# Last quarter of the residual and last head's queries computed by features; arriving tiles in buffers of their own

## The chip, the core and the metric

The kernel runs on one core of one Trainium2 chip. The metric is the device time of one execution in microseconds; the runs given are the median of three, with the lowest and highest. All inputs and outputs are float32.

## What is computed

One encoder block over 256 rows of 2048 features, with a second input of 256 memory rows. Cut to its core:

```python
h = rms_norm(x, norm_g[0])
q, k, v, g, lr, u_f, u_h, u_s = jnp.split(h @ w_in, split_at, axis=-1)
mix = concat([gla(...), rms_norm(fnet(u_f)), rms_norm(hyena(u_h)), rms_norm(shortconv(u_s))])
x = x + mix @ w_out                                                     # 2048 -> 2048
x = x + cross_attention(rms_norm(x, norm_g[1]), mem_n, w_xq, w_xkv, w_xo)
x = x + swiglu(rms_norm(x, norm_g[2]), w_gate_up, w_down)               # 2048 -> 2 x 5632 -> 2048
return rms_norm(x, final_norm_g)

def cross_attention(h, mem_n, w_q, w_kv, w_o):                          # 4 heads of 512
    q = h @ w_q;  k, v = split(mem_n @ w_kv)
    p = softmax(q k^T * 512 ** -0.5);  return (p v) @ w_o
```

## The kernel before

**Three matmuls for one product.** Every float32 operand is split in a high part (a copy to the type fp32r, by ScalarE) and a low part (the difference, by VectorE). A product is high x high + high x low + low x high. A weight block is 128 x 128; weights come in slabs of 16 blocks (1 MB) by one SyncE queue, in the order in which they are used, and are split half a slab (8 blocks) at a time: `Stream._half`, L104 on ScalarE and L105 on VectorE. A half is cast up to two or three halves ahead of its use; the buffers are three (four while `st.extra` is open). Activations lie as 128 features x 256 rows, high part and low part beside each other in one tile of 512 columns: `act[0..23]` and, for a while, others.

**By rows, by features.** A gemm has two forms. By rows (`gemm_rows`, `part_rows`, L347 to L349): the activation is the stationary operand, four weight blocks side by side are the moving one, and the result in PSUM is 128 rows x 512 output features, for each half of the 256 rows. For a group of four blocks that is six matmuls of 512 columns. By features (`gemm`, `mm`, L298 and L299): the weight block is stationary, the activation moves (high and low in one matmul of 512 columns, then the low weights with the high activation, 256 columns), and the result is 128 output features x 256 rows, in two halves which `merge` adds: a copy by ScalarE and an add by VectorE. For four blocks that is eight matmuls, of 3072 columns in all like the six.

**Turning.** A result by rows has its features along the free axis, and the next gemm wants them on partitions. So it is turned: VectorE transposes 32 x 32 blocks (`store_turned`, L382), GpSimd's queue stores the tile to DRAM (L384), and later loads it with the blocks put in their places (`load_turned`, L389). This is done for the residual after `w_out` and after `w_xo` (`features1`, `features2`), for the queries (`queries`), the keys and the MLP's hidden activations. The weights' rows are permuted on the host to fit (`turned`).

**Background work.** While the gemms are written out, small pieces of other work are put between the matmuls by `Background`: each is a generator that yields the time, in microseconds of matmul time counted by the program, after which it may go on. `arrive(src, c, put, ok)` is the piece of this change: it takes four temporaries of 128 x 256, issues the four loads of quarter c, yields 9.0, waits for `ok`, and then splits the four tiles (`put`). Each engine runs its own instructions in order, so a split that is queued too early stands at the head of its engine's queue until its tile has landed, and whatever comes behind it, weight splits too, stands with it. GpSimd's queue too is in order: a load waits there for its stores to land, and what is behind waits as well. The temporaries are a pool of 11 (`tmp`).

**The stages around the change**, in the order in which they run:

- `out_proj`: `w_out` by rows in quarters of 512 features, the first two together, then the third, then the fourth. After each, `add_rows` adds the result into the residual `res[c]` (rows x 512 features), turns and stores it, and squares it on ScalarE for the row norm (`sq`). The slots of `act[16:24]` hold the mixers' output until `w_out` ends, and take the third and fourth quarter of the next input `h2` then.
- `attention`: `w_xq` by rows, one head of 512 queries at a time; each is stored, loaded and split into `q` tiles (eight buffers). Keys and values come from DRAM as `mr` tiles (`load_kv`), and are split into `kt`, `vh`, `vl`. `head` does scores (L776, L777), softmax, and probabilities by values (L803, L804). The first `w_xq` gemm runs over k in parts, 0 to 7, 8 to 11 and 12 to 15, each part behind the arrival of its slots. `row_norm(0)` sums `sq` for the scale.
- `w_xo` by rows, again two quarters together, then one, then one; the third input `h3` arrives as `h2` did.
- `gate_up` and `down`: the MLP, by rows. The first gate_up gemm takes k 0 to 11, then 12 to 15. The final norm needs the residual at the end; its fourth quarter is put into two PSUM banks early (L872: the residual split in two, times the identity `identr`, held through gate_up), and `w_down`'s last quarter is added onto it there.

The lists `late` and `self.late` hold the arrivals; `drain` writes out what is left of one.

Of the kernel before, what the change touches and what calls it, by code (L numbers as in the profile page):

```python
# [22 lines left out]
P = 128  # L23
# [15 lines left out]
ROWS = ((0, 512), (704, 768), (880, 944), (1152, NBLK))  # L39
# [3 lines left out]
LAG, OWED, SOON = 1.3, 0.9, 0.01  # L43
# [19 lines left out]
class Stream:  # L63
# [13 lines left out]
    def _half(self):  # L77
# [24 lines left out]
        edges = [0, 256, 512, 1024] if n == 0 else [0, 512, 1024] if n == 8 else [0, 1024]  # L102
# [69 lines left out]
class Block:  # L172
# [219 lines left out]
    def run(self):  # L392
# [9 lines left out]
        self.identr = cp.tile([P, P], F32R, name="identr")  # L402
# [28 lines left out]
        nc.gpsimd.tensor_copy(self.identr, self.ident)  # L431
        with self.tc.tile_pool(name="wx", bufs=1) as st.extra:
            self.mixers()
            self.attention()
# [6 lines left out]
    def mixers(self):  # L441
# [79 lines left out]
        with tc.tile_pool(name="mid", bufs=1) as mid:  # L521
# [37 lines left out]
            with tc.tile_pool(name="glp", bufs=1) as glp:  # L559
# [13 lines left out]
                self.out_proj(lambda n: self.bg.drain((g_gla, g_sc, g_fn)[n]))  # L573
# [63 lines left out]

    def row_norm(self, n, box):

        self.bg.dve(8)  # L640
        c = self.rp.tile([P, 8], F32, name="sm", tag="sm")[:, 0:2]
        self.nc.vector.tensor_reduce(out=c, in_=self.sq[n].rearrange("p (r k) -> p r k", k=4), axis=AX.X, op=ALU.add)
        box["col"] = self.rstd_cols(c, D)

    def out_proj(self, before):
        nc, act = self.nc, self.act

        def ready(n):

            if n:  # L650
                before(n - 1)
                for c in ((2, 3), (1,), (0,))[n - 1]:
                    for r in range(2):
# [3 lines left out]
        slots = act[4:8] + act[0:4] + act[16:24]  # L657
        h2 = self.h2 = act[8:24]
        put = lambda k, t: self.split_scaled(h2[k], t, self.gvec(V_NG + 16, k))
        free = self.st.n + 192 + 32  # L660
        self.late = []

        def done(c, ps):
            self.add_rows(0, c, ps)
            self.late.append(self.bg.add(self.arrive(self.xf[0], c, put, c > 1 and (lambda: self.st.n >= free)), go=True))

        for c, ps in enumerate(self.gemm_rows("w_out", [0, 512], slots, parts=[range(k, k + 4) for k in (8, 0, 12, 4)], before=ready)):
            done(c, ps)
# [3 lines left out]
    def attention(self):  # L672
        tc, nc, act, st = self.tc, self.nc, self.act, self.st
        with tc.tile_pool(name="atp", bufs=1) as atp, tc.tile_pool(name="kp", bufs=1) as kp, \
# [4 lines left out]
            self.gap(vp, 128)  # L679
            oex = [atp.tile([P, 512], F32R, name=f"oex{i}") for i in range(4)]  # L680
# [13 lines left out]
            heads = []  # L694
# [37 lines left out]
            def scores(hd):  # L732
                q = []

                def put(k, t):
                    q.append(slot("q", 8))
                    self.split(q[-1], t)

                yield from self.arrive(self.qf, hd, put, lambda: len(heads) > hd - 2)
                while len(kv[hd][2]) < 2:  # L740
                    yield
                yield
                yield from self.head(q, *kv[hd], pt, o[4 * hd:4 * hd + 4], qs)
# [4 lines left out]
            late = self.late  # L748
            for hd in range(4):
                first = dict(parts=[range(8), range(8, 12), range(12, 16)],  # L750
                             before=lambda n: [self.bg.drain(g) for g in late[:n + 2]]) if hd == 0 else {}
                for r, p in enumerate(self.gemm_rows("w_xq", [hd * 512], self.h2, **first)[0]):
# [3 lines left out]
            self.late = []  # L756
            put = lambda k, t: self.split_scaled(h3[k], t, self.gvec(V_NG + 32, k))

            def done(c, ps):
                self.add_rows(1, c, ps)  # L760
                self.late.append(self.bg.add(self.arrive(self.xf[1], c, put), go=True))

# [771 lines left out]
```

## Time and profile before

| | |
|---|---|
| runs | 1490.69, 1495.62, 1498.5 us; median 1495.62 us |
| profiled execution | 1493.05 us, its span 1491.2 us |
| mean granted TensorE clock | 0.996 |
| instructions in the span | 18456 |
| DMA | 315.46 MB, mean 212 GB/s |
| GpSimd's queue: stores of residual / loads of residual | 32 / 32, 128 KB each |
| GpSimd's queue: stores of queries / loads of queries | 16 / 16, 128 KB each |

The span runs from the first to the last instruction; the time is a little longer. Times below are microseconds from the span's start. A row of the timeline gives start, duration, engine, line, operation, and in brackets the engine's idle time before it with what ended it. PE is TensorE's matmuls, PEld its weight loads, which overlap them, ACT ScalarE, DVE VectorE, POOL GpSimd and SP SyncE. The stages: `w_out` runs from about 457 to 551, the queries and heads from there, `w_xo` from about 662 to 764 (its first part with the last heads between), `gate_up` behind it to about 1243, and `down` to the end.

### The profile page before, as it was taken

To read this page: it belongs to the slowest core of one execution; us is meant where nothing else is said; L and a number is where in the kernel's file an instruction comes from. 1 tells how busy PE (TensorE), PEld (TensorE's weight loads), DVE (VectorE), ACT (ScalarE), POOL (GpSimd) and SP (SyncE) were. 2 spreads that over 40 slices of the span, in tenths; PEclk is the share of its full clock that TensorE was granted. 3 is DMA by queue.
4 is the path that set the end of the run, shared out by engine and by line. 5 is a ranking of instruction groups with operands and counts; after the bars stand their busy time and mean duration, and the time that the engine had idled before them with its cause. 6 is when DMAs were issued, how large, how long until landed. Compare 5 with 4: busy or idle time off the path is not lost.

```text
span 1491.2 us, 18456 instructions
## 1 busy us (share of the span) xinstructions
PE 1468.3 (98%) x6960; PEld 1223.7 (82%) x6960; DVE 926.5 (62%) x1324; ACT 752.1 (50%) x1092; POOL 172.3 (12%) x229
## 2 busy tenths in 40 slices
PE   9999999999999999999999999999999999999997
PEld 7887888898898877788878888888888888888886
DVE  6668768779767565776664545555554556444444
ACT  6557655467555454665554444444444445444344
POOL 0000000000001324340331001111100111000000
PEclk9999999999999999999999999999999999999999
DMA  9776654454536767774676667666666666555554
GB/s 357 279 273 244 212 203 156 165 185 155 194 141 219 241 210 244 219 218 149 223 244 207 212 212 225 219 216 219 219 214 213 225 214 220 191 194 197 197 195 144
DMA packets 58441, 315.46 MB, mean 212 GB/s; under 512 B 8781, under 2 KB 10478, under 8 KB 26736
## 3 DMA queue, kind: packets, MB, share of 16 engines
q1 hardware_dynamic: 46496, 281.11, 54.9%
q0 software_dynamic: 11424, 32.52, 8.3%
q8 instruction: 54, 0.88, 0.3%
q10 hardware_dynamic: 432, 0.66, 0.1%
q14 instruction: 35, 0.29, 0.1%
HBM read 295.90 MB, written 18.35 MB: 211 GB/s over the span
## 4 chain that ended last, share of the span: by engine, by line
PE 84%; DMA 6%; issue 5%; DVE 2%; POOL 2%; ACT 1%; SPq 0%; POOLq 0%; DVEq 0%; ACTq 0%
PE pg L348 21%; PE pg L347 21%; PE pg L349 21%; PE pg L298 6%; PE pg L299 4%; DMA tmp<-features 2%; DMA features<-tmp 2%; PE pm L349 1%; PE pm L347 1%; PE pm L348 1%; DVE wl L105 1%; PE pg L295 1%; PE pg L296 1%; PE pm L1028 1%; POOL tmp L389 1%
## 5 line engine op out<-in xcount | busy, mean ns | idle before, releaser
L105 DVE TENSOR_TENSOR wl<-raw,wh 128x1024 fp32r<-128x1024 f32 (+1 forms) x503 | 610.2, 1216 | 449.4 <-ACT wh L104 448.2
L104 ACT CAST wh<-raw 128x1024 fp32r<-128x1024 f32 (+1 forms) x503 | 522.8, 1042 | 546.0 <-PE pg L349 456.3
L347 PE MATMUL pg<-wh,act 128*128 128x512 f32 (+1 forms) x1522 | 594.5, 391 | 6.6 <-ACT wh L104 4.0
L348 PE MATMUL pg<-wl,act 128*128 128x512 f32 (+1 forms) x1522 | 593.6, 390 | 3.0 <-DVE wl L105 3.0
L349 PE MATMUL pg<-wh,act 128*128 128x512 f32 (+1 forms) x1522 | 592.9, 390 | 0.4 <-DVE act L204 0.4
L347 PEld LDWEIGHTS pg<-wh,act 128*128 128x128 f32 x1522 | 286.0, 188 | 69.8 <-ACT wh L104 5.2
L348 PEld LDWEIGHTS pg<-wl,act 128*128 128x128 f32 x1522 | 286.0, 188 | 64.8 <-DVE wl L105 6.4
L349 PEld LDWEIGHTS pg<-wh,act 128*128 128x128 f32 x1522 | 286.0, 188 | 61.0 <-DVE act L204 1.5
L299 PE MATMUL pg<-act,wl 128*128 128x256 f32 x512 | 143.5, 280 | 0.0
L298 PE MATMUL pg<-act,wh 128*128 128x512 f32 x400 | 141.2, 395 | 0.0
L299 PEld LDWEIGHTS pg<-act,wl 128*128 128x128 f32 x512 | 96.3, 188 | 0.3
L298 PEld LDWEIGHTS pg<-act,wh 128*128 128x128 f32 x400 | 75.2, 188 | 16.2
L384 POOL DMA_DIRECT2D hidden<-u x22 | 16.7, 762 | 387.1 <-DVE u L382 387.1
L347 PE MATMUL pg<-wh,f 128*128 128x512 f32 x120 | 46.7, 389 | 0.0
L348 PE MATMUL pg<-wl,f 128*128 128x512 f32 x120 | 46.7, 389 | 0.0
L349 PE MATMUL pg<-wh,f 128*128 128x512 f32 x120 | 46.7, 389 | 0.0
L389 POOL DMA_DIRECT2D tmp<-hidden x44 | 38.8, 888 | 39.5 <-ACT wh L104 17.1
L384 POOL DMA_DIRECT2D features<-tmp x32 | 22.7, 715 | 113.0 <-DVE tmp L382 112.5
L204 DVE SCALAR_TENSOR_TENSOR act<-tmp,vec,act 128x256 fp32r<-128x256 f32 x32 | 14.7, 481 | 33.7 <-ACT act L212 33.7
L212 ACT ACTIVATE act<-tmp,vec 128x256 fp32r<-128x256 f32 x32 | 15.4, 504 | 37.2 <-DMA tmp<-features 37.1
L389 POOL DMA_DIRECT2D mr<-keys x16 | 14.2, 890 | 154.1 <-DVE act L200 148.1
L389 POOL DMA_DIRECT2D tmp<-features x32 | 28.1, 885 | 31.2 <-DMA features<-tmp 19.9
(295 smaller groups left out, 1239.2 us busy)
## 6 DMA issues: line engine op xcount, KB each, us to landing
raw<-in_W SPq DMA_DIRECT2D x246, 1024.0 KB, 5.1
raw<-in_W SPq DMA_DIRECT2D x11, 512.0 KB, 7.4
hidden<-u POOLq DMA_DIRECT2D x22, 256.0 KB, 3.6
tmp<-hidden POOLq DMA_DIRECT2D x44, 128.0 KB, 4.9
features<-tmp POOLq DMA_DIRECT2D x32, 128.0 KB, 3.6
tmp<-features POOLq DMA_DIRECT2D x32, 128.0 KB, 5.2
k<-in_mem SPq DMA_DIRECT2D x8, 256.0 KB, 9.0
keys<-k POOLq DMA_DIRECT2D x8, 256.0 KB, 7.2
```

What stands on the lines that cost most here:

```text
L104: nc.scalar.copy(wh[:, a:b], r[:, a:b])
L105: nc.vector.tensor_tensor(out=wl[:, a:b], in0=r[:, a:b], in1=wh[:, a:b].bitcast(F32), op=ALU.subtract)
L212: self.nc.scalar.activation(slot[:, 0:R], src, AF.Copy, scale=g)
L295: self.nc.tensor.matmul(p[:, 0:R], wh, slot[:, 0:R], start=start, stop=False)
L296: self.nc.tensor.matmul(p[:, 0:R], wh, slot[:, R:512], start=False, stop=False)
L298: self.nc.tensor.matmul(p[:, :], wh, slot[:, :], start=start, stop=False)
L299: self.nc.tensor.matmul(p[:, 0:R], wl, slot[:, 0:R], start=False, stop=stop)
L347: self.nc.tensor.matmul(p, hi, wh, start=start, stop=False)
L348: self.nc.tensor.matmul(p, hi, wl, start=False, stop=False)
L349: self.nc.tensor.matmul(p, lo, wh, start=False, stop=stop)
L384: self.nc.gpsimd.dma_start(to[r], u.rearrange("p (k c) -> p k c", c=P))
L389: self.nc.gpsimd.dma_start(t.rearrange("p (g t) -> p g t", t=32), src)
```

## The change

1. The fourth quarter of `w_out` and of `w_xo` is computed by features (`add_features`, L298 and L299): four columns of 16 blocks, each merged and added onto `resk(12 + i)`, which now holds that quarter of the residual as 128 features x 256 rows, loaded from `xT` at the start. No turn, store or load. Squares are summed over the four tiles, and `row_norm` sums them over the partitions with two matmuls by a column of ones. Their splits read the sum in place.
2. The fourth head's queries are computed by features too; the merged tiles are split into `act[12:16]` at its turn. The `q` buffers are four instead of eight, and a head's queries may be split as soon as the head before has been scored.
3. `arrive` takes its tiles from buffers of their own (eight `ar` tiles in `attention`, four in `gate_up`; the third quarter after `w_out` uses `tmp` still), and yields 18.0 (`FAR`) instead of 9.0 between loads and splits. The third quarter after `w_out` is split only when all of `w_out` has been issued.
4. The third quarter after `w_xo` is loaded from the start of `gate_up`, with 11.0 before its splits; the first gate_up gemm runs over k in the parts 0 to 7, 8 to 11 and 12 to 15.
5. The fourth quarter is put into the two PSUM banks only before `down`, by eight transposes; `identr` goes.
6. The third and fourth half slab of the kernel are split in two pieces each (`n < 32`), as the first two were.
7. The weights' permutations and the placement of weight tiles (`ROWS`) follow.

```diff
-ROWS = ((0, 512), (704, 768), (880, 944), (1152, NBLK))
+ROWS = ((0, 512), (704, 768), (880, 944), (1152, 1344), (1408, 1600), (1664, 1856), (1920, NBLK))
-LAG, OWED, SOON = 1.3, 0.9, 0.01
+LAG, OWED, SOON, FAR = 1.3, 0.9, 0.01, 18.0
...
-        edges = [0, 256, 512, 1024] if n == 0 else [0, 512, 1024] if n == 8 else [0, 1024]
+        edges = [0, 256, 512, 1024] if n == 0 else [0, 512, 1024] if n < 32 else [0, 1024]
...
-    def arrive(self, src, c, put, ok=None):
+    def arrive(self, src, c, tile_, put, wait, ok=None):
         m = []
         for k in range(4 * c, 4 * c + 4):
-            m.append(self.tmp())
+            m.append(tile_())
             self.load_turned(m[-1], src, k)
-        yield 9.0
+        yield wait
...
+    def add_features(self, w, slots, h, g):
+        nc = self.nc
+        def add(i, p):
+            x = self.resk(12 + i)
+            self.tt(x, x, self.merge(p), ALU.add)
+            s = self.tmp()
+            nc.scalar.activation(s, x, AF.Square)
+            if i:
+                self.tt(s, self.sqf, s, ALU.add)
+            self.sqf = s
+        def rest():
+            for k in range(12, 16):
+                self.split_scaled(h[k], self.resk(k), self.gvec(g, k))
+                yield SOON
+        self.gemm(w, [1536 + i * P for i in range(4)], slots, add)
+        return self.bg.add(rest())
+
     def row_norm(self, n, box):
-        self.bg.dve(8)
+        nc = self.nc
+        p = self.bank()
+        for r in range(2):
+            nc.tensor.matmul(p[:, r:r + 1], self.sqf[:, r * P:(r + 1) * P], self.ones[:, 0:1], start=True, stop=True)
+        self.bg.dve(8, 2)
...
+        nc.vector.tensor_reduce(out=c, in_=self.sq[n].rearrange("p (r k) -> p r k", k=4)[:, :, 0:3], axis=AX.X, op=ALU.add)
+        self.tt(c, c, p[:, 0:2], ALU.add)
...
+                    if c == 3:
+                        self.load_x(12, 4)
+                        continue
...
-        for c, ks in ((2, [range(16)]), (3, [range(8, 16), range(8)])):
-            done(c, self.gemm_rows("w_out", [c * 512], slots, parts=ks)[0])
...
+            arrival = lambda: mp.tile([P, R], F32, name="ar", tag="ar", bufs=8)
+            free = self.st.n + 128
...
+                late.append(self.bg.add(self.arrive(self.xf[0], c, self.tmp if c > 1 else arrival, put, FAR, c > 1 and (lambda: self.st.n >= free)), go=True))
+            done(0, ps[0])
+            done(1, ps[1])
+            done(2, self.gemm_rows("w_out", [1024], self.mix)[0])
+            late.append(self.add_features("w_out", self.mix, h2, V_NG + 16))
...
-                    q.append(slot("q", 8))
+                    q.append(act[k] if hd == 3 else slot("q", 4))
...
-                yield from self.arrive(self.qf, hd, put, lambda: len(heads) > hd - 2)
-                while len(kv[hd][2]) < 2:
+                if hd == 3:
+                    for k in range(12, 16):
+                        put(k, last[k - 12])
+                        yield SOON
+                else:
+                    yield from self.arrive(self.qf, hd, arrival, put, FAR, lambda: len(scored) >= hd)
+                while len(kv[hd][2]) < 2 or len(heads) < hd:
                     yield
...
-            for hd in range(4):
+            for hd in range(3):
...
+            last = []
+            self.gemm("w_xq", [1536 + i * P for i in range(4)], h2, lambda i, p: last.append(self.merge(p)))
+            self.bg.add(scores(3), go=True)
...
-            for c in (2, 3):
-                done(c, self.gemm_rows("w_xo", [c * 512], o)[0])
-                st.extra = None
+            self.add_rows(1, 2, self.gemm_rows("w_xo", [1024], o)[0])
+            st.extra = None
+            self.late = self.add_features("w_xo", o, h3, V_NG + 32)
+            for g in late:
+                self.bg.drain(g)
...
-        ps = self.gemm_rows("w_gate_up", [0, DFF], self.h3, parts=[range(12), range(12, 16)],
-                            before=lambda n: n and [self.bg.drain(g) for g in self.late])
-        self.bg.drain(pre)
-        for r in range(2):
-            for i in range(2):
-                nc.tensor.matmul(self.end[r][:, :], self.identr, f[2 * r + i], start=i == 0, stop=False)
+        arrival = lambda: gp.tile([P, R], F32, name="ar", tag="ar", bufs=4)
+        ready = [self.bg.add(self.arrive(self.xf[1], 2, arrival, self.put3, 11.0), go=True), self.late]
+        col = self.bg.add(norm())
+        ps = self.gemm_rows("w_gate_up", [0, DFF], self.h3, parts=[range(8), range(8, 12), range(12, 16)],
+                            before=lambda n: n and self.bg.drain(ready[n - 1]))
...
+        end = [self.bank() for _ in range(2)]
+        mark = self.mark()
+        for r in range(2):
+            for j in range(4):
+                nc.tensor.matmul(end[r][:, j * P:(j + 1) * P], self.resk(12 + j)[:, r * P:(r + 1) * P], self.ident,
+                                 is_transpose=True, start=j == 0, stop=False)
+        self.keep_place(mark)
```

More of the change, by code (lines that the diff above doesn't have):

```diff
@@ L652, in ready, with attention @@
                 for c in ((2, 3), (1,), (0,))[n - 1]:
+                    if c == 3:
+                        self.load_x(12, 4)
+                        continue
                     for r in range(2):
                         nc.sync.dma_start(self.half(c, r), self.t["x"][r * P:(r + 1) * P, c * 512:(c + 1) * 512])
[L657 to L668, printed above, removed]
-        for c, ks in ((2, [range(16)]), (3, [range(8, 16), range(8)])):
-            done(c, self.gemm_rows("w_out", [c * 512], slots, parts=ks)[0])
-    def attention(self):
+        self.mix = act[4:8] + act[0:4] + act[16:24]
+        return self.gemm_rows("w_out", [0, 512], self.mix, parts=[range(k, k + 4) for k in (8, 0, 12, 4)], before=ready)
+    def attention(self, ps):
         tc, nc, act, st = self.tc, self.nc, self.act, self.st
@@ L853, in fetch, with norm @@
                     yield pause
-        self.end = [self.bank() for _ in range(2)]
-        def rows():
+        def norm():
             yield 2.0
@@ L1476 @@
     vecs[:, V_NG:V_NG + 48] = col(x["norm_g"])
-    vecs[:, V_NG + 16:V_NG + 48] = turned(vecs[:, V_NG + 16:V_NG + 48])
+    for c in (16, 32):
+        vecs[:, V_NG + c:V_NG + c + 12] = turned(vecs[:, V_NG + c:V_NG + c + 12])
     vecs[:, V_GRP:V_GRP + 12] = col(x["grp_norm_g"])
```

45 lines of the change are left out of this document (22 added, 23 removed).

## The prediction

> **What bounds the kernel now.** I read the page's busy times first, then who waited for whom on PE, then windows around each wait, then the timelines of PE and ACT inside them.
>
> ```profile
> ## 1 busy us (share of the span) xinstructions
> PE 1468.3 (98%) x6960; PEld 1223.7 (82%) x6960; DVE 926.5 (62%) x1324; ACT 752.1 (50%) x1092; POOL 172.3 (12%) x229
> ```
>
> TensorE works for 98% of the span, so a change pays only through PE: fewer or cheaper matmuls, or PE's own stops removed. PE's waits between 500 and 780 us (output projection, attention, attention's output projection) are few and all trace to the two engines that feed it:
>
> ```profile
> PE pg L347 <- ACT wh L104: 3.6, 2, 2.0
> PE pg L347 <- ACT act L212: 2.6, 2, 1.5
> PE pg L348 <- DVE wl L105: 2.4, 4, 0.8
> PE pm L776 <- ACT q L208: 2.2, 1, 2.2
> PE pg L349 <- DVE act L204: 0.4, 1, 0.4
> ```
>
> The columns are total us, times, longest. L104 and L105 split the weights, L212 and L204 the arriving residual, L208 the arriving queries. The windows (stretch, length, PE busy, matmuls, granted clock, DMA share, GB/s) put the stops in five places; the last row, the rest of the MLP, has none:
>
> ```profile
> 526.00:550.00 24.00, 21.59 (x93) 1.00 0.67 219
> 564.00:576.00 12.00, 8.96 (x36) 1.00 0.52 151
> 594.00:607.00 13.00, 10.76 (x34) 0.74 0.75 177
> 738.00:748.00 10.00, 9.15 (x40) 1.00 0.56 165
> 757.00:763.00 6.00, 3.26 (x13) 1.00 0.21 42
> 822.00:1466.00 644.00, 644.00 (x2842) 1.00 0.64 211
> ```
>
> ACT's timeline at the first stop shows the cause: after the weight cast of 535.31 ACT stands at the first split of an arriving tile until its DMA lands, and the next weight cast, which needs none of it, runs only at 546.73.
>
> ```profile
> 535.31 1.05 ACT L104 CAST wh<-raw 128x1024 fp32r<-128x1024 f32 x1 [1.71 <-PE pg L349]
> 542.55 0.51 ACT L212 ACTIVATE act<-tmp,vec 128x256 fp32r<-128x256 f32 x1 [6.19 <-DMA tmp<-features]
> 545.20 0.51 ACT L212 ACTIVATE act<-tmp,vec 128x256 fp32r<-128x256 f32 x1 [2.14 <-DMA tmp<-features]
> 546.73 1.03 ACT L104 CAST wh<-raw 128x1024 fp32r<-128x1024 f32 x1
> ```
>
> PE pays there twice, for the high and for the low half:
>
> ```profile
> 545.77 0.39 PE L349 MATMUL pg<-wh,act 128*128 128x512 f32 x1
> 547.81 0.50 PE L347 MATMUL pg<-wh,act 128*128 128x512 f32 x1 [1.65 <-ACT wh L104]
> 549.07 0.50 PE L348 MATMUL pg<-wl,act 128*128 128x512 f32 x1 [0.76 <-DVE wl L105]
> ```
>
> **What the stops cost.** PE's undisturbed start-to-start distance in this form is 0.227 us (541.23 to 543.95 holds 12). Excess over it, from the starts: first stop 2.04 + 1.26 + 0.34 - 3 x 0.227 = 3.0 us. Second (starts 565.11 to 574.28, with steps of 1.84, 1.56 and 0.81): 3.9. Third: from 595.51 to 605.88 PE does eight query-key pairs (0.34 each) and six row matmuls, 4.1 us of work in 10.4: 6.3 lost, of which 2.2 is the wait and about 4 is what follows it, since the granted clock reads 0.50 from 600 to 604. Fourth (740.61, 746.70): 1.4. Fifth (757.26 to 761.23): 3.3. Sum 17.9 us. All stand behind residual or query tiles that land later than ACT reaches them.
>
> **The change, part by part.**
>
> (1) Later splits. A quarter's splits are now queued 18 us of matmul time after its loads are issued (was 9). In the trace a residual load landed 8.3 us after issue at most, and POOL waited 6.8 us at most for the stores before it: 15.1, inside 18. The third quarter of the first projection waits for that projection's end, 64 blocks x 0.3475 = 22.2 us after its stores begin; in the trace its stores at 530.64 had the last split at 547.66, 17.0 later. The third quarter of the second projection is loaded from the start of gate_up (the built order, counted in matmul time, has its loads on POOL right behind its stores, and its splits 11.8 us into gate_up); eight of sixteen k come first, 8 x 2.72 = 21.8 us. The tiles' own buffers keep them from holding shared temporaries meanwhile. Stops one, four and five, which are second and third quarters, go.
>
> (2) Last quarter by features, twice. It needs no turn, store and load: 4 + 4 POOL DMAs less each. Its splits read the sum in place. Its chain after the last column is an ACT copy (0.41), two DVE adds (0.42 each), a Square (0.50) and a split (0.50 + 0.48), some 3 us; the next gemm needs it after 12 k, 16.3 us (in gate_up 32.6). Stop two, the first projection's last quarter, goes. Extra work, 4 copies, 4 Squares and 11 DVE adds against 2 row Squares, 2 wide adds and 4 turns, is about 2 us each on ACT and DVE in 22 us; it lies beside matmuls (ACT 50% busy, DVE 62%) and costs nothing while casts stay ahead.
>
> (3) Last head's queries by features: 8 POOL DMAs less, nothing to wait for. Heads 0 to 2 wait 18 us too, so in the built order head 0's scores stand 30.6 us behind its query gemm instead of 18 (577.43 to 595.51 in the trace). Stop three goes, with its slow stretch.
>
> (4) PE's price of the features form. Two of its matmuls at the old place:
>
> ```profile
> 400.26 0.39 PE L298 MATMUL pg<-act,wh 128*128 128x512 f32 x1
> 400.49 0.28 PE L299 MATMUL pg<-act,wl 128*128 128x256 f32 x1
> 400.61 0.39 PE L298 MATMUL pg<-act,wh 128*128 128x512 f32 x1
> ```
>
> Four pairs from 399.91 to 401.30: 0.3475 us a block, 1.390 for four, against 6 x 0.2267 = 1.360 by rows. 3 x 16 groups of four x 0.030 = +1.4 us.
>
> (5) Two sums of squares through PE: four fp32 matmuls of one column. L246 is that form: 16 rows from 430.29 to 432.00, two rows to an instruction: 4 x 0.214 = +0.9. They stand in PE's queue and wait for DVE's last add with a gemm behind them; in the built order they come 5 us after the last column, against a chain of about 4, so I add no wait.
>
> (6) The end: four identity matmuls of 512 columns (0.93) become eight fp32 transposes (L795: four in 0.36): -0.2. (7) At the start two more weight halves are split in two: PE waited 0.31 over its pace at 13.27 for a whole low half; bounds 0 to -0.5 (that and its neighbours), taken -0.3.
>
> Sum without new waits: -17.9 + 1.4 + 0.9 - 0.2 - 0.3 = -16.1. **New waits** are the unknown: bounds 0 and 6.3 (the dearest stop of the trace). I take 2.0: at the borders between forms a PSUM bank is emptied by copy plus add (0.83) just before it is written again, twice, and the key tiles below may cost a little. -14.1 from the profiled execution's 1493.05 (span 1491.2 and 1.9 around it) is 1479.0; from the median of the runs, 1495.62, it is 1481.5. I say **1480**.
>
> On what a short stop costs, the row is stop three: 2.19 us of idle, then 0.50 of the clock. The Trainium skill (TensorE: Matmul & The Clock Gate, "Why this matters for your kernels") asks only that PE's idle gaps stay under some 3 us. By it a new wait of that length costs 2.2 and the sum's upper bound shrinks by 4; the trace disagrees, and the bound stays 6.3.
>
> **Rivals.** *Keys in the queries' place.* Second and later key tiles of head 1 are loaded behind the queries' loads on POOL. In the trace the first such tile landed at 598.65, 21.2 us after the gemm's end at 577.43, and held ACT (1.37 at 598.68). The new order has ACT reach one 14.6 us after the gemm: 6.6 us of standing. PE ran 9.8 us on what was cast (536.36 to 546.16) before it felt a stop; with a cast due every 2.72, some 7 is covered. Against: the DMA share was about 1.0 there, behind stop two, and head 1's queries, with no stop before them, landed theirs in 2.2 to 3.0 us. If it bites, it delays casts and scores: 4 more, 1484.
>
> *Stops move.* The same number of tiles still passes through POOL and ACT; if half of the 17.9 reappears elsewhere (9), 1489. Against: the built order leaves 15 us or more between load and split almost everywhere.
>
> *Weight loads come into the open.* By features there are eight loads per four blocks, by rows six; if the two more were paid in full, 96 x 0.188 = 18 us and 1498. Against: a pair takes 0.3475 us with two loads of 0.188, which would not fit end to end. The Trainium skill (TensorE: Matmul & The Clock Gate, "The mechanism") says loads overlap matmuls only across row groups; by it this rival holds, and the pair's row speaks against it.
>
> *Slower: every operand moves.* Dropping the 512-byte identity copy shifts all weight and activation tiles behind it by 512 bytes a partition. Should PE's reads depend on place so that row matmuls pace like the features form (1.390 for 1.360, 2.2%), 1400 us cost 31 more: 1511. It decides from the first gemm on. Against: the three or four weight buffers lie at different places now and pace alike.
>
> **How the numbers follow.** Forecast 0.66, keys 0.18, moved stops 0.08, weight loads 0.03, shifted operands 0.05. A measurement can tell 0.5% (7.5 us), so faster means under 1488.1: 0.66 + 0.18 + half of 0.08 = 0.88; same 0.04 + 0.03 = 0.07; slower 0.05. Range: no new wait and the full start gain, -16.3, from the lowest run (1490.69) is 1474; new waits of 6.3, -9.8, from the highest (1498.5) is 1489.
>
> **What would show it.** Right: PE busy in every window from 526 to 763; no L212 or L208 wait of ACT over 2 us; features pairs at 0.3475; rows at 0.2267; clock 1.00 throughout. Wrong: an ACT wait on key or query tiles with a PE wait behind it, a clock dip near 600, a PE wait at the row-norm matmuls or at a bank's first matmul after a features gemm, or another pace in the MLP's untouched stretch.

## The result and the profile after

The changed kernel takes 1476.61 us (median of six runs, 1475.65 to 1477.61) against 1492.37 for the kernel before (median of six, the three on which the prediction stands among them): a ratio of the means of 0.9889, 95% interval 0.9869 to 0.9909. Its profiled execution has a span of 1475.6 us, 15.6 less than before, and the mean granted clock is 0.999.

From the page of the changed kernel, the busy times and the shares of the chain that ended last:

```profile
PE 1463.1 (99%) x7068; PEld 1227.5 (83%) x7068; DVE 930.6 (63%) x1336; ACT 754.5 (51%) x1104; POOL 152.9 (10%) x204
...
PE 97%; DVE 1%; ACT 0%; DMA 0%; issue 0%; SPq 0%; DVEq 0%
```

TensorE's idle time in the span fell from 22.9 to 12.5 us; its busy time fell by 5.2 too, though it has 108 matmuls more, and part of that is the old slow stretch behind stop three, where the granted clock was 0.50. The chain is TensorE almost throughout. What PE waited for in the whole span (total us, times, longest):

```profile
PE pm L1069 <- DVE w3l L200: 1.2, 2, 0.8
PE pg L347 <- ACT wh L104: 1.2, 2, 0.9
PE pm L423 <- DVE eps L424: 1.1, 1, 1.1
PE pg L348 <- DVE wl L105: 0.5, 2, 0.2
PE pg L347 <- ACT g L870: 0.4, 1, 0.4
```

No arriving tile is among them, neither residual nor queries. The windows on the five old stops, moved to where the same work stands now (stretch, length, PE busy, ..., granted clock, DMA share, GB/s), and the rest of the MLP:

```profile
526.00:550.00 24.00, 24.00 (x136) 20.94 (x135) 19.82 (x36) 17.12 (x34) 6.35 (x8) 1.00 0.77 233
561.00:573.00 12.00, 12.00 (x54) 9.93 (x54) 7.73 (x13) 6.54 (x10) 4.40 (x7) 1.00 0.74 236
582.00:598.00 16.00, 16.00 (x73) 13.23 (x72) 8.75 (x17) 8.96 (x16) 8.02 (x12) 1.00 0.85 222
720.00:732.00 12.00, 12.00 (x64) 10.31 (x63) 8.49 (x16) 7.55 (x15) 6.36 (x8) 1.00 0.84 251
736.00:748.00 12.00, 12.00 (x70) 10.55 (x69) 8.73 (x15) 7.29 (x12) 0.00 (x0) 1.00 0.62 198
806.00:1450.00 644.00, 644.00 (x2847) 533.35 (x2846) 334.85 (x337) 279.77 (x316) 50.42 (x60) 1.00 0.63 210
```

PE is busy without a break at clock 1.00 in all. Where the time went is read by cutting each span at three rows of GpSimd's queue that both kernels have: the first store of the residual, the first and the last store of the MLP's hidden tiles.

| us | start to first residual store | to first hidden store | to last hidden store | to the end |
|---|---|---|---|---|
| before | 502.70 | 307.51 | 436.04 | 244.99 |
| after | 503.13 | 291.13 | 435.82 | 245.50 |
| difference | +0.43 | -16.38 | -0.22 | +0.51 |

All of the gain lies in the second stretch, from the projections to the first MLP gemm.

The keys' rival left its mark on ScalarE. Its timeline in the changed kernel (start, duration, engine, line, operation, and the idle time before it with what ended it):

```profile
582.55 1.05 ACT L104 CAST wh<-raw 128x1024 fp32r<-128x1024 f32 x1 [1.37 <-PE pg L349]
589.99 0.41 ACT L208 CAST kt<-mr 128x256 fp32r<-128x256 f32 x1 [6.39 <-DMA mr<-keys]
590.30 1.04 ACT L104 CAST wh<-raw 128x1024 fp32r<-128x1024 f32 x1
```

ACT stood 6.39 us at a key tile, and 7.75 us passed between the starts of two weight casts. The window 582 to 598 above shows that PE felt nothing. PE's timeline in `add_features`, for the price of the form by features:

```profile
533.68 0.39 PE L298 MATMUL pg<-act,wh 128*128 128x512 f32 x1
533.91 0.28 PE L299 MATMUL pg<-act,wl 128*128 128x256 f32 x1
...
535.07 0.39 PE L298 MATMUL pg<-act,wh 128*128 128x512 f32 x1
```

Four blocks from 533.68 to 535.07: 1.39 us, as predicted.

### The profile page after: what moved, and what is told of

It is laid out like the page before. It is cut to its first block, busy times and chain, and to the rows that moved or that the text cites. A ratio compares the mean times of both kernels' runs of the same rounds, so it can differ in the third digit from the quotient of the medians.

```text
span 1475.6 us, 18641 instructions
## 1 busy us (share of the span) xinstructions
PE 1463.1 (99%) x7068; PEld 1227.5 (83%) x7068; DVE 930.6 (63%) x1336; ACT 754.5 (51%) x1104; POOL 152.9 (10%) x204
## 4 chain that ended last, share of the span: by engine, by line
PE 97%; DVE 1%; ACT 0%; DMA 0%; issue 0%; SPq 0%; DVEq 0%
PE pg L347 24%; PE pg L349 24%; PE pg L348 24%; PE pg L298 9%; PE pg L299 6%; PE pm L349 1%; PE pm L348 1%; PE pm L347 1%; PE pg L295 1%; PE pg L296 1%; PE pm L1069 1%; PE pm L843 1%; PE pm L815 0%; DMA raw<-in_W 0%; PE pm L1450 0%
## 5 line engine op out<-in xcount | busy, mean ns | idle before, releaser
L105 DVE TENSOR_TENSOR wl<-raw,wh 128x1024 fp32r<-128x1024 f32 (+2 forms) x505 | 611.6, 1213 | 464.3 <-ACT wh L104 462.9
L104 ACT CAST wh<-raw 128x1024 fp32r<-128x1024 f32 (+2 forms) x505 | 523.9, 1039 | 567.8 <-PE pg L349 469.3
L347 PE MATMUL pg<-wh,act 128*128 128x512 f32 (+1 forms) x1434 | 559.7, 390 | 1.6 <-ACT wh L104 1.2
L348 PE MATMUL pg<-wl,act 128*128 128x512 f32 (+1 forms) x1434 | 558.0, 389 | 0.6 <-DVE wl L105 0.5
L349 PE MATMUL pg<-wh,act 128*128 128x512 f32 (+1 forms) x1434 | 558.0, 389 | 0.0
L347 PEld LDWEIGHTS pg<-wh,act 128*128 128x128 f32 x1434 | 269.2, 188 | 59.8 <-ACT wh L104 1.8
L349 PEld LDWEIGHTS pg<-wh,act 128*128 128x128 f32 x1434 | 269.2, 188 | 56.1
L298 PE MATMUL pg<-act,wh 128*128 128x512 f32 x576 | 202.9, 394 | 0.0
L299 PE MATMUL pg<-act,wl 128*128 128x256 f32 x688 | 192.7, 280 | 0.0
L299 PEld LDWEIGHTS pg<-act,wl 128*128 128x128 f32 x688 | 129.4, 188 | 0.4
L298 PEld LDWEIGHTS pg<-act,wh 128*128 128x128 f32 x576 | 108.2, 188 | 23.5
L295 PE MATMUL pg<-act,wh 128*128 128x256 f32 x112 | 31.7, 283 | 0.0
L296 PE MATMUL pg<-act,wh 128*128 128x256 f32 x112 | 31.4, 281 | 0.0
L389 POOL DMA_DIRECT2D mr<-keys x16 | 14.1, 888 | 152.2 <-DVE act L200 148.1
```

Source lines behind the costliest of these rows:

```text
L104: nc.scalar.copy(wh[:, a:b], r[:, a:b])
L105: nc.vector.tensor_tensor(out=wl[:, a:b], in0=r[:, a:b], in1=wh[:, a:b].bitcast(F32), op=ALU.subtract)
L295: self.nc.tensor.matmul(p[:, 0:R], wh, slot[:, 0:R], start=start, stop=False)
L296: self.nc.tensor.matmul(p[:, 0:R], wh, slot[:, R:512], start=False, stop=False)
L298: self.nc.tensor.matmul(p[:, :], wh, slot[:, :], start=start, stop=False)
L299: self.nc.tensor.matmul(p[:, 0:R], wl, slot[:, 0:R], start=False, stop=stop)
```

## The experiments

Times are medians with the lowest and highest run. The middle stretch is the second column of the table above. A "stretch without a cast" is the distance between the starts of two following L104 casts on ACT in the timeline; a cast is due every 2.7 us. From one group of runs to the next the median of the kernel before moved between 1491.81 and 1493.15, so differences of about 1 us between medians of different groups say nothing.

**One number alone.** The kernel before with

```diff
-        yield 9.0
+        yield 18.0
```

> The kernel before with one number changed: arriving tiles are queued for their splits 18.0 instead of 9.0 us of matmul time after their loads; temporaries, forms, everything else as before. In the built order load and split of the tiles then stand 14 us or more apart, except in the last quarter of the first projection (8 to 9.5, since the first query gemm needs it). Lateness theory (the stops are splits queued before their tile has landed): stops one, three, four and five of the prediction go (3.0 + 6.3 + 1.4 + 3.3 = 14.0), stop two stays at 3.9; 1492.4 - 14.0 = 1478.4, within 3. Rival, transfers (the query and residual tiles are late because the last quarter's stores and loads and the fourth head's stand in the same queue, and only the form by features takes them away): stops two and three stay, 10.2, and the time is 1492.4 - 7.7 = 1484.7 or more.

Measured: 1476.35 us (1475.29 to 1478.05), ratio 0.9895 (0.988 to 0.9909); the middle stretch takes 289.49. Its windows at the first three stops:

```profile
526.00:550.00 24.00, 24.00 (x108) 19.87 (x107) 17.54 (x28) 14.05 (x22) 6.35 (x8) 1.00 0.88 269
561.00:573.00 12.00, 12.00 (x54) 9.93 (x53) 9.48 (x16) 6.95 (x12) 3.08 (x5) 1.00 0.83 245
582.00:598.00 16.00, 16.00 (x73) 13.23 (x72) 9.84 (x16) 9.23 (x18) 8.24 (x13) 1.00 0.92 247
```

All five stops are gone, the second too, which was to stay. ACT's timeline at the last quarter's tiles:

```profile
563.04 1.01 ACT L212 ACTIVATE act<-tmp,vec 128x256 fp32r<-128x256 f32 x2
564.45 0.51 ACT L212 ACTIVATE act<-tmp,vec 128x256 fp32r<-128x256 f32 x1 [0.40 <-DMA tmp<-features]
```

The tiles landed 562.61 to 565.13, from 12.3 us after their first store at 550.31 on, and ACT came to them at 563.04 and stood 0.6 us in all; before, it came 7.6 us after the first store. So this one number gives what the whole change gives, without a form by features and without buffers of their own for the tiles. The removal of transfers is not needed for it.

**The changed kernel without that number.**

```diff
-LAG, OWED, SOON, FAR = 1.3, 0.9, 0.01, 18.0
+LAG, OWED, SOON, FAR = 1.3, 0.9, 0.01, 9.0
```

> The changed kernel with 9.0 instead of 18.0 between loads and splits; forms by features, own tiles and the later third quarter of the second projection stay. Lateness theory: ACT reaches the second quarter of both projections 4.5 to 5.4 us and head 0's queries 7.5 us after the loads in the built order, and they landed later than that; stop one (3.0), stop four (1.4) and a part of stop three (3 to 6.3) come back, stops two and five do not: 1476.6 + 7.4 to 10.7 = 1484 to 1487. Rival, transfers: with the last quarter's and the fourth head's transfers gone the rest lands early enough, no more than 2 us come back: under 1479.

Measured: 1479.65 us (1478.93 to 1481.06), ratio 0.9917 (0.9902 to 0.9932); middle stretch 293.02. Only 3.0 us came back, between the two expectations. The middle stretch is 1.9 longer than the changed kernel's, and two waits of PE make up 1.8 of it:

```profile
PE pm L835 <- DVE tmp L829: 1.1, 1, 1.1
PE pg L299 <- DVE wl L105: 0.7, 1, 0.7
```

ACT stood 6.17 us at the second quarter (9.2 us without a cast), and PE 0.70 for it. The longer wait, at 600.41, is for head 0's softmax. It comes behind ACT's stands at head 0's queries (2.59) and at keys (1.79, 1.31), the last of them at 591.66; that these caused it is not shown. The rest of the change alone is worth some 12.5 us: gain and causes overlap.

**Residual later, queries not.** The kernel before with 18.0 for the residual's tiles and 9.0 for the queries.

```diff
-    def arrive(self, src, c, put, ok=None):
+    def arrive(self, src, c, put, ok=None, wait=18.0):
...
-        yield 9.0
+        yield wait
...
-                yield from self.arrive(self.qf, hd, put, lambda: len(heads) > hd - 2)
+                yield from self.arrive(self.qf, hd, put, lambda: len(heads) > hd - 2, 9.0)
```

> The kernel before with 18.0 between loads and splits for the residual's tiles alone; the heads' queries keep 9.0 (in the built order head 0's splits stand 5.9 to 8.8 us behind their loads, closer than in the kernel before). Between the first store of the residual and the first store of the MLP's hidden tiles the kernel before took 307.5 us, the changed kernel 291.1, the kernel before with 18.0 everywhere 289.5. Theory as the prediction had it (stop three is head 0's queries landing later than ACT reaches them, by themselves): 6.3 stay, 289.5 + 6.3 = 295.8, time about 1482. Rival, knock-on (the queries were late because stop two had made the weight stream catch up beside their stores and loads): without stop two they land some 10 us after their loads, ACT stands for 3 to 5 us, less than it is ahead of PE, and the stretch takes 290 to 291, the time 1476 to 1478.

Measured: 1477.87 us (1475.64 to 1482.2), the profiled execution the longest (span 1480.4); middle stretch 294.35, 4.9 more than with 18.0 everywhere. ACT's timeline in it, then PE's rows with a wait, then the window behind them (granted clock 0.72):

```profile
578.04 1.05 ACT L104 CAST wh<-raw 128x1024 fp32r<-128x1024 f32 x1 [1.36 <-PE pg L349]
...
586.84 0.41 ACT L208 CAST q<-tmp 128x256 fp32r<-128x256 f32 x1 [7.13 <-DMA tmp<-queries]
587.15 1.04 ACT L104 CAST wh<-raw 128x1024 fp32r<-128x1024 f32 x1
```

```profile
588.55 0.50 PE L776 MATMUL pm<-kt,q 128*128 128x512 f32 x1 [0.41 <-ACT q L208]
589.84 0.38 PE L777 MATMUL pm<-kt,q 128*128 128x256 f32 x1 [0.79 <-DVE q L200]
592.32 0.39 PE L777 MATMUL pm<-kt,q 128*128 128x256 f32 x1 [1.09 <-DVE q L200]
```

```profile
592.00:598.00 6.00, 5.68 (x20) 4.74 (x21) 4.86 (x13) 3.15 (x7) 1.09 (x2) 0.72 0.97 354
```

Without stop two ACT still stood 7.13 us at head 0's queries, and the scores behind them stopped PE for 2.3 us in three pieces, with a lower clock behind them. So in this execution the queries were late by themselves, and the knock-on falls. The median speaks the other way: it lies in the range of the knock-on (1476 to 1478). The runs spread over 6.6 us and only the longest was profiled, so how often the queries come too late is open.

**Keys by age, and keys sooner.** First, a key or value tile of the changed kernel is split only 12 us of matmul time after its load:

```diff
-LAG, OWED, SOON, FAR = 1.3, 0.9, 0.01, 18.0
+LAG, OWED, SOON, FAR, AGE = 1.3, 0.9, 0.01, 18.0, 12.0
...
-                        parts.append(m)
+                        parts.append((m, self.bg.now))
...
+                    while self.bg.now < parts[n][1] + AGE:
+                        yield
...
```

> The changed kernel with a key or value tile split only when 12 us of matmul time have passed since its own load was issued. It takes away ACT's one long stand, 6.4 us at the first late key tile of head 1. Theory (the stand is covered by what is cast ahead): the stand is gone or under 2 us and the time stays, 1476.6 within 1. Rival (the stand delays head 1's scores and the casts behind it, and costs up to the 4 us that the prediction put on it): 1473 to 1475.

Measured: 1477.81 us (1476.68 to 1478.22), ratio 0.9904 (0.9888 to 0.9921). The 6.4 us stand is gone (the longest left is 1.25), and nothing is gained. Then the opposite:

```diff
-                    yield 1.0
+                    yield SOON
```

> The changed kernel with the key and value tiles split at once one after another (the pause of 1.0 us of matmul time between two tiles gone). In the built order the first late key tile of head 1 stands 5.4 us earlier for ACT, its load at the same place behind the queries' loads. Cover theory (ACT's stand costs PE only what exceeds the weights cast ahead, about 7 us): ACT stands 10 to 12 us instead of 6.4, PE stops for 3 to 5 us near 590, with the clock falling behind it perhaps, and the time is 1480 to 1485. Rival (PE does not hang on that stand at all): a stand of 10 to 12 us and no PE stop, 1476.6 within 1.

Measured: 1477.74 us (1476.74 to 1479.99), middle stretch 292.32, 1.2 more than the changed kernel's. ACT's timeline, and PE's rows with a wait:

```profile
575.22 1.05 ACT L104 CAST wh<-raw 128x1024 fp32r<-128x1024 f32 x1 [1.06 <-PE pg L349]
...
584.95 0.41 ACT L208 CAST kt<-mr 128x256 fp32r<-128x256 f32 x1 [7.02 <-DMA mr<-keys]
585.26 1.04 ACT L104 CAST wh<-raw 128x1024 fp32r<-128x1024 f32 x1
```

```profile
586.35 0.50 PE L347 MATMUL pg<-wh,act 128*128 128x512 f32 x1 [0.29 <-ACT wh L104]
587.61 0.50 PE L348 MATMUL pg<-wl,act 128*128 128x512 f32 x1 [0.76 <-DVE wl L105]
```

The tile landed 5.0 us earlier than in the changed kernel's profile, where everything from the start on stood 1.9 us later, so the stand grew by less than expected and the time lies between the two expectations; but 10.0 us without a cast stopped PE for 1.05. The 7.75 us of the changed kernel lay inside what is cast ahead.

**A smaller lead.** Weights cast two half slabs ahead instead of three from the queries on.

```diff
-            ahead = self.n // 8 + 1 + min(3 if self.extra else 2, self.n // 16)
+            ahead = self.n // 8 + 1 + min(3 if self.extra and self.n < 1408 else 2, self.n // 16)
```

> The changed kernel with weights cast at most two half slabs ahead of their use instead of three from the queries' gemms on; every split of an arriving tile stays where it is. Cover theory: ACT still stands about 6.4 us at the first late key tile of head 1, but PE has 2.7 us less cast in front of it, so it stops there for 2 to 3 us, followed perhaps by up to 4 us at half clock; 1479 to 1483. Rival (the stand does not reach PE because nothing there needs it): no stop near 590, 1476.6 within 1.

Measured: 1477.2 us (1476.2 to 1479.52). In the profiled execution the keys landed in time and ACT did not stand there at all (1.81 us at a value tile was the longest), so this tells nothing of the lead.

**Between 9 and 18.** The kernel before with `yield 12.0`:

> The kernel before with 12.0 instead of 9.0 between loads and splits, a third of the way to 18.0; nothing else. In the built order the distances grow by 2 to 4 us (second quarters 6.1 to 6.8 us, third 9 to 10, head 0's queries 10 to 11.6). Cover theory (a stand of ACT costs PE only what exceeds some 6.5 us; the stands of before, alone or close together, were 5.5 to 9 us, just above): stands of 3 to 6 us remain and nearly all the gain is there, 1476 to 1479. Rival (a stop shrinks by as much as the split is moved): a third of 15.8 is gained, about 1487.

Measured: 1496.33 us (1493.33 to 1499.39), ratio 1.003 (1.0015 to 1.0044): slower than at 9.0. Both expectations fell. What PE waited for from 500 to 850 us:

```profile
PE pm L776 <- ACT q L208: 3.5, 2, 2.9
PE pg L347 <- DVE res L200: 3.0, 1, 3.0
PE pg L347 <- ACT act L212: 2.3, 1, 2.3
```

Three stops of over 2 us, each with the clock at 0.50 to 0.52 for two microseconds or more behind it; before, one of the five stops had that. ACT still stood 33.2 us at residual tiles (37.1 before), in other pieces. The longest stop, 2.99 us at 765.49, stands behind no long stretch without a cast (the casts are at 753.01, 758.69 and 762.55): PE waits there for the residual's adds, which stood on DVE behind a weight split. Temporaries that the longer wait keeps could do the rest, but the loads do not show it: GpSimd waited 3.0 us between two loads of the third quarter after `w_xo`, but 3.06 at the same place with 9.0. The changed kernel, most of whose tiles have their own buffers, was run at 12.0:

> The changed kernel with 12.0 between loads and splits, the number at which the kernel before became slower than at 9.0 (1496.3). In all profiles so far PE stood for nothing when ACT went up to 8.6 us without a weight cast, and nearly always when it went 9 us or more. Theory (the changed kernel has no such stretch left, because the last quarters and the fourth head's queries do not arrive by the queue and the tiles have buffers of their own): stretches under 9 us, 1476.6 to 1479.7, between its times at 18.0 and at 9.0. Rival (at 12.0 a split of a second quarter falls among the weight casts at a worse place, whatever the form of the last quarter): a stretch of 9 us or more, 1482 or more.

Measured: 1483.78 us (1480.3 to 1486.2), ratio 0.9925 (0.9898 to 0.9952): by the medians 4 slower than at 9.0, 7 than at 18.0. The runs at 9.0 and 12.0 are of different groups and their ratios to the kernel before overlap; in the profiles the middle stretch takes 296.60 against 293.02. Own buffers do not cure it. Rows of ACT, DVE and PE at its largest stop, and the window over it (granted clock 0.74):

```profile
519.83 1.05 ACT L104 CAST wh<-raw 128x1024 fp32r<-128x1024 f32 x1 [0.86 <-PE pg L349]
528.61 1.03 ACT L104 CAST wh<-raw 128x1024 fp32r<-128x1024 f32 x1
531.63 1.03 ACT L104 CAST wh<-raw 128x1024 fp32r<-128x1024 f32 x1
```

```profile
532.17 1.28 DVE L200 TENSOR_TENSOR res<-res,pg 128x512 f32<-128x512 f32 x2
533.36 1.41 DVE L382 STREAM_TRANSPOSE tmp<-res 128x256 f32<-128x256 f32 x4
534.70 2.32 DVE L105 TENSOR_TENSOR wl<-raw,wh 128x1024 fp32r<-128x1024 f32 x2
```

```profile
535.94 0.38 PE L299 MATMUL pg<-act,wl 128*128 128x256 f32 x1 [1.94 <-DVE wl L105]
```

```profile
534.00:540.00 6.00, 4.06 (x16) 3.50 (x17) 5.97 (x10) 3.73 (x7) 3.19 (x5) 0.74 0.66 223
```

The stand at the second quarter (8.8 us without a cast) falls later here than at 9.0, and the third quarter's end comes before the casts have caught up: the low half of the cast of 531.63 waits behind the residual's adds and transposes until 534.70, and PE until 535.94. At 9.0 the same stand ended 2.9 us earlier (516.4 to 525.7 without a cast) and cost 0.70; at 18.0 it is not there.

**The start.** The changed kernel with the start's splits as before:

```diff
-        edges = [0, 256, 512, 1024] if n == 0 else [0, 512, 1024] if n < 32 else [0, 1024]
+        edges = [0, 256, 512, 1024] if n == 0 else [0, 512, 1024] if n == 8 else [0, 1024]
```

> The changed kernel with the weight halves at the start split as before (the third and fourth half slab whole). The prediction gave the finer split -0.3 us; in the one profile of the changed kernel the first store of the residual stands 0.4 us later than before, behind a second slab that landed at 9.48 instead of 8.43 us. If that is the landing alone, this kernel takes 1476.6 + 0.3, within 0.5, and its second slab lands anywhere between the two; if the finer split itself costs (two more instructions on each engine, a later slab by a later release of its buffer), 1476.2 or less and the second slab near 8.4.

Measured: 1477.5 us (1475.7 to 1479.75), just outside both expectations, with runs 4 us apart; in the profiled execution, the longest, the second slab's first half landed at 9.87 us. And the kernel before with 18.0 and the finer start:

```diff
-        yield 9.0
+        yield 18.0
...
-        edges = [0, 256, 512, 1024] if n == 0 else [0, 512, 1024] if n == 8 else [0, 1024]
+        edges = [0, 256, 512, 1024] if n == 0 else [0, 512, 1024] if n < 32 else [0, 1024]
```

> The kernel before with 18.0 everywhere and, at the start, the third and fourth half slab split in two as in the changed kernel; nothing by features. The stretches of the profiles say that the forms by features cost about 1.6 us between the residual's first store and the hidden tiles' first store and 0.5 at the end, less 0.6 in gate_up; so, start apart, this kernel is 1.5 us faster than the changed one: 1475 (within 1.5), against 1476.6. Rival (the forms by features are worth their price somewhere that the one profile does not show): 1476.6 or more.

Measured: 1476.18 us (1474.92 to 1478.04), ratio 0.9886 (0.9869 to 0.9904); the landing at 9.02; middle stretch 291.00, 1.5 more than in the other kernel with the same middle. The expected 1.5 us of advantage can't be told from that scatter, and no version measured beats the changed kernel by more than it. The landing of that load, which is issued at 2.6 us in every kernel, varies over all profiled executions from 7.87 to 9.92. It sets the start only in part: the first store of the residual stood latest, at 505.3, behind two of the three latest landings (9.87 and 9.92), but at 503.88 behind one of 7.93 (the changed kernel at 12.0) and at 502.70 behind one of 8.43 (before). Windows of the kernel before with 18.0, where it landed at 9.92, from 11 to 15 us:

```profile
11.00:13.00 2.00, 1.77 (x5) 1.36 (x5) 1.59 (x4) 1.88 (x4) 0.00 (x0) 0.63 1.04 406
13.00:15.00 2.00, 2.00 (x6) 1.53 (x5) 1.94 (x3) 1.53 (x4) 0.00 (x0) 0.52 1.07 418
```

PE stands 1.28 us for the slab, until 10.61, and then runs at about half clock to 15.0. With the landing at 9.48 (the changed kernel) it stood 0.90 and kept the clock.

**What a stop does to the clock.** Ten stops of set length in gate_up of the changed kernel:

```diff
...
+    def idle(self, n):
+        nc, p, t = self.nc, self.bank(), self.tmp()
+        mark = self.mark()
+        nc.tensor.matmul(p[:, 0:R], self.onesr, self.h3[0][:, 0:R], start=True, stop=True)
+        nc.scalar.copy(t, p[:, 0:R])
+        for _ in range(n):
+            nc.scalar.copy(t, t)
+        nc.tensor.matmul(p[:, 256:257], t[:, 0:P], self.ones[:, 0:1], start=True, stop=True)
+        self.keep_place(mark)
```

> The changed kernel with ten stops of PE put into gate_up, each in the middle of a gemm: a matmul, 3, 5, 7, 9 or 13 copies on ACT in a row that follow from it, and a matmul that follows from the last copy; twice through these five lengths. At 0.31 to 0.42 us a copy PE stands about 1.2, 2, 2.8, 3.5 and 5 us. The time says nothing; the granted clock behind each stop does. Theory A (a threshold between 1 and 2 us of a single stop, as the start shows: 0.90 us left the clock at 1.00, 1.28 was followed by 4 us near 0.5): 0.5 behind all but the shortest. Theory B (the Trainium skill, TensorE: Matmul & The Clock Gate, asks only for gaps under some 3 us): 0.5 behind the two longest alone. Theory C (it hangs on more than the stop's length: the trace of before has stops of 1.65 and 1.98 with the clock at 1.00 behind them and one of 2.19 with 0.50): no length parts them, and equal stops go either way.

The first attempt answers nothing: the gemm's other matmuls were put ahead of the waiting one, and PE stood 0.23 us at most. With them held behind it, and 0, 1, 2, 4 and 8 further copies:

```diff
+        mark = self.mark()
...
+        if self.pin:
+            self.keep_place(mark)
+            self.pin -= 1
...
+        self.pin = 24
```

> As the ten stops before, with the matmuls behind each held in their order, so that PE truly stands: a matmul, 1, 2, 3, 5 or 9 copies on ACT in a row, and a matmul that needs the last; twice through these lengths, in the middle of ten gemms of gate_up. A first copy begins about 0.9 us behind its matmul and each further one takes 0.31 to 0.41, so PE stands some 1.3, 1.7, 2.1, 2.9 and 4.5 us. Read is the granted clock in the 5 us behind each stop. A (one threshold between 0.9 and 1.28 us, as at the start): half clock behind all. B (the Trainium skill, TensorE: Matmul & The Clock Gate: gaps under some 3 us are harmless): half clock behind the 4.5 us stops alone. C (more than the length decides): equal stops go either way.

Measured stops: 1.29, 1.73, 2.16, 3.04 and 4.78 us, then 1.29, 1.73, 2.16, 3.03 and 4.78. Windows behind the first five (the last three columns are granted clock, DMA share, GB/s):

```profile
827.00:831.00 4.00, 4.00 (x19) 3.25 (x19) 0.56 (x2) 1.05 (x1) 0.00 (x0) 1.00 0.47 197
873.00:877.00 4.00, 4.00 (x19) 3.29 (x18) 0.19 (x1) 1.05 (x1) 0.00 (x0) 1.00 0.36 150
919.00:923.00 4.00, 4.00 (x11) 3.23 (x12) 0.00 (x0) 0.00 (x0) 0.00 (x0) 0.50 0.28 119
969.00:973.00 4.00, 3.92 (x12) 3.16 (x13) 0.00 (x0) 0.02 (x1) 0.00 (x0) 0.60 0.19 80
1020.00:1024.00 4.00, 4.00 (x10) 3.18 (x11) 0.00 (x0) 0.00 (x0) 0.00 (x0) 0.50 0.00 0
```

Up to 1.73 us the clock stays, from 2.16 on it halves, and the second five went the same way (0.62 in the four microseconds behind the second stop of 2.16). But the kernels' own stops show no one border. The 1.94 us of the changed kernel at 12.0 halved the clock (0.50 from 537 to 540), while the 1.98 us at the fifth stop of the kernel before left it at 1.00. With the queries at 9.0 and the residual at 18.0, three stops of 0.41, 0.79 and 1.09 us within 4 us were followed by 0.50 from 593 to 596. At the start 1.28 and 1.29 were enough in two executions, with stops of 0.15 to 0.42 and 0.23 us just before, while 1.34 in a third (this kernel's own start, the landing at 9.91) left the clock at 1.00. So the first two readings fall, and the third holds for the kernels' own stops: near 2 us in the steady part and near 1.3 at the start, nearly equal stops went either way. Whether stops lie close together does not settle it either, since 0.76 us more followed the 1.98 within 1.3 us. What else decides was not tried.

## Why the prediction was right, and where it was not

- *The five stops go, 17.9 us.* Right. Their windows are full at clock 1.00, and the middle stretch is 16.38 us shorter. By the prediction's terms that stretch should lose 17.9, gain 1.4 and 0.9, and lose the 0.9 of the old identity matmuls: -16.5 without new waits.
- *New waits, taken as 2.0.* This is the term that was mis-sized: they are about nothing (one wait of 0.4 us, at L870, in the whole stretch). Neither the banks at the borders between forms nor the row norm's matmuls show one. It accounts for 2.0 of the 3.4 us between 1480 and 1476.6. Most of the rest is the base: 1480 with the sum's -14.1 starts from 1494.1, and the median of the six runs of before is 1492.37.
- *Parts 2 and 3, the forms by features remove stop two and help with stop three.* They do remove the transfers, but they are not what the gain needs: the step "stop two, the first projection's last quarter, goes" holds without them, since the later splits also took ACT to that quarter 12.7 us after its first store instead of 7.6. Part 1, the 18 us, carries the prediction; with it undone 3.0 us come back, since the other parts keep most stands short by another way.
- *Stop three includes about 4 us of half clock.* The mechanism is shown by the stops of set length: 2.16 us halved the clock twice. The Trainium skill (TensorE: Matmul & The Clock Gate, "Why this matters for your kernels") would have let that stop pass, and the runs disagree.
- *Rival, keys in the queries' place.* On ACT it came true as worked out (6.6 us predicted, 6.4 measured), and it cost nothing: the 4 us that the rival put on it did not come, and the cover of some 7 us, which the prediction set against it, held. In all profiles ACT went up to 8.6 us without a cast and PE did not wait for weights; at 9.0 to 10.0 it stood 0.5 to 2.7, for weights or for the late tiles themselves, at 11.1 and 11.4 in the kernel before 3.0 and 2.4. At 12.0 in the changed kernel 8.8 led to 1.94, late, because other work of ACT and DVE came before the casts had caught up.
- *Price of features, +1.4.* Right by its rows, 1.39 for four blocks. *Row norm, +0.9:* 0.36 a norm by its rows, and 0.09 more because the matmul behind it takes longer to its successor: 0.9 for the two. *The end, -0.2:* eight transposes take 0.79 against 0.93; they are new in the last two stretches, which together are 0.3 longer.
- *Start, -0.3.* Measured +0.4, with a landing that varies by 2 us whatever the splits. Its own price stays open.
- *Moved stops, weight loads in the open, moved operands.* None is seen: PE stands nowhere in the middle but for the 0.4 us named above, pairs take 0.3475, and 644 us of the MLP are full in both kernels, at 0.2267 a matmul.

The prediction set 18 us against the sum of the latest landings, 15.1, and said nothing of what lies between 9 and 18; that less than the full move does harm (12.0 is worse than 9.0 in the kernel before, and by its medians and profiles in the changed one) was seen neither there nor in the expectation for the kernel before; for the changed kernel it stood as the rival. Left open is why 12.0 costs the kernel before as much as it does, and what the finer start is worth.

## What to carry to other kernels

In an in-order engine that feeds another, look at the distance between two feeds, not at the length of one wait: here 8.6 us without a cast were free and 9.0 were not. At stops one, four and five PE stood for weights behind such a stretch, at two and three for the late tiles themselves; one number removed all five, 18 us. It is not the whole account: at 12.0 PE stopped 1.94 us behind 8.8 and 2.99 behind none over 5.7, because of other work queued between cast and use. Before rebuilding a transfer, try the one number that says when its consumer is queued, and try more than one value: in the kernel before too little was worse than nothing. A stop that halves the clock costs more than its length (1.7 and 2.3 times at the two set stops of 2.16 us, 2.9 times at stop three), so look at the granted clock behind it.

## What the hardware showed that was not expected

A set stop of 2.16 us halved TensorE's clock both times, 1.73 neither time; of the kernels' own, one of 1.94 us did it and one of 1.98 did not, three of at most 1.09 us within 4 us did, and at the start 1.28 and 1.29 us did it and 1.34 did not. Behind the first stop of 2.16 us 14 matmuls in a row began 0.43 us apart, behind the second 7. The first 512 KB of the second slab, issued at 2.6 us into the span, landed anywhere from 7.9 to 9.9 us, and the first store of the residual stood anywhere from 501.2 to 505.3.
